# A fourth Toeplitz buffer, rotation tables from two short runs, an earlier weight split and a later spread in a two-layer decoder trunk

## The chip, the cores and the metric

The program runs on one core of a Trainium2 chip. The metric is the device time of one execution in microseconds (us). The kernel before was timed at 2249.5, 2243.65 and 2248.94 us, median 2248.94; a separate execution was profiled and took 2244.88 us. TensorE (PE) multiplies matrices, VectorE (DVE), ScalarE (ACT) and GpSimd (POOL) work elementwise, and SyncE (SP) issues most of the transfers between device memory and the on-chip buffers. Each engine, and each engine's issue queue, works in the order of its own list: what waits holds back all that stands behind it.

## The reference

Two layers, each a mixer and a dense feed-forward block (FFN) with RMS norms and residual adds. The same weights serve a prompt of 1024 positions and 8 samples of 8 positions with carried state; the kernel lays both side by side as 1088 columns. All work is float32. Layer 0 mixes with a convolution module, layer 1 with a diagonal state-space scan (SSM):

```python
def conv_module(h, buf, w_pw1, b_pw1, w_dw, b_dw, ln_g, ln_b, w_pw2):
    a = h @ w_pw1 + b_pw1
    v = a[..., :D_MODEL] * jax.nn.sigmoid(a[..., D_MODEL:])
    full = jnp.concatenate([buf.astype(v.dtype), v], axis=1)
    y = lax.conv_general_dilated(full, w_dw[:, None, :], ..., feature_group_count=D_MODEL) + b_dw
    y = jax.nn.silu(layer_norm(y, ln_g, ln_b))
    return y @ w_pw2, full[:, -(CONV_WIDTH - 1):]
...
def swiglu(h, w_gate, w_up, w_down):
    return (jax.nn.silu(h @ w_gate) * (h @ w_up)) @ w_down
...
yp = yp + dp
yp = yp + swiglu(rms_norm(yp, norm_ffn[i]), w_gate[i], w_up[i], w_down[i])
```

The scan of layer 1 needs, for each of 64 groups and 64 state rows (kept as 128 lanes), powers of a complex number of unit size: 128 cosines and 128 sines per group. The kernel tabulates them while layer 0 runs; they are called rotations.

## The kernel before, in words

*Tiles.* A tile has 128 partitions and up to 1088 columns. Most large tiles (named `big`) come from one pool of 35 slots that are handed on as they come free. Weights of the pointwise products are fetched into 3 `w` slots and split into a high and a low half (`split_weight`: ScalarE writes the high half, VectorE the low one) in 6 `wg` slots; a product is then three matmuls for each 128x128 piece, high by high, high by low and low by high.

*The convolution stage* loops over channel blocks fb = 0 to 7 of 128 channels, and `depthwise` follows two blocks behind. `pointwise(fb)` makes two products (`pv`, `pg`; 72 matmuls each) and gates one with the other into `v`. `relayout(fb)` sends `v` through device memory (`vs`, then `u`) into a layout in which the depthwise convolution is a product with Toeplitz tiles. `depthwise(fb)` runs 80 matmuls `dw` with four such tiles `tz` (640 KB each, three slots); the result goes back through device memory (`ys`) into `y`. `moments` adds up the sums over blocks that the layer norm needs (`lnsum`, `lnsq`): blocks 0 to 3 are summed by VectorE and TensorE then makes the mean (`lcps`, in the middle of the product of block 7), while blocks 4 to 7 are summed in the transposed layout (`late_moments`: `late4` to `late7`, added up in `late4_0`), so that their sums can be taken (`late`, line 1218) as soon as the last depthwise product is done.

*Beside it* runs the preparation of the SSM: `ssm_parameters`; `replicate_powers`, 32 transfers `edup` issued on ScalarE's queue; and `rotations(fb)`. For each block, 44 GpSimd instructions double a run of cosines and sines from 1 to 128 entries, and two stores (`st_tc`, `st_ts`, 512 KB each, SyncE's queue) write them out.

*The second pointwise product* takes the normalised tiles `n0` to `n7` (`h` and `l` halves). Output blocks 0 to 2 are computed together, column chunk by column chunk, while the layer norm is applied; blocks 3 to 7 follow one after another (`p`), each with its own split weight. `skip_products` (line 530) puts eight copies `xrep` on ScalarE in that place. `Mixed` gathers the sums for the FFN's RMS norm, and `spread` turns the factor per column into a tile `f0r` by a product (`f0rp`) with a diagonal `f0rdg` that GpSimd makes.

*Order.* The program is written as loops and a scheduler orders each engine's list by its own cost model; `later(n)` lowers the priority of what is written under it, and `issue_after` adds an order between two instructions.

Of the kernel before, what the change touches and what calls it, by code (L numbers as in the profile page):

```python
# [8 lines left out]
F32 = mybir.dt.float32  # L9
F32R = mybir.dt.float32r  # L10
# [4 lines left out]
P = 128  # L15
D = 1024
# [3 lines left out]
L = 8  # L20
# [42 lines left out]
def decoder_kernel(ctx: ExitStack, tc: tile.TileContext, A):  # L63
# [46 lines left out]
        SP.dma_start(w, src)  # L110
        return w, name

    def split_weight(w, name, behind=None, ordered=False):
        wh = wpool.tile([P, D], F32R, tag="wg", name=f"{name}h", bufs=6)
        high = S.activation(wh, w, AF.Copy)
        if ordered:
            tc.keep_in_program_order(high)
        wl = wpool.tile([P, D], F32R, tag="wg", name=f"{name}l", bufs=6)
        with tc.issue_after(behind.ins) if behind else nullcontext():
            V.tensor_sub(wl, w, wh.bitcast(F32))  # L120
        return wh, wl
# [412 lines left out]
    def skip_products():  # L534
# [18 lines left out]
        ssm["dg"] = cpool.tile([P, G], F32, name="dg")  # L553
        V.tensor_mul(ssm["dg"], cst[:, K_DREP : K_DREP + G], cst[:, K_GREP : K_GREP + G])

    def rotations(fb):

        gs = slice(fb * GF, (fb + 1) * GF)
        tcos, tsin, t1 = [big(f"rot{fb}_{i}") for i in range(3)]
        cv, sv, tmp = [t[:, :D].rearrange("p (g n) -> p g n", n=NCK) for t in (tcos, tsin, t1)]  # L560
        GP.tensor_copy(cv[:, :, 0], ssm["zc"][:, 0, gs])
        GP.tensor_copy(sv[:, :, 0], ssm["zs"][:, 0, gs])
        for lv in range(NLV):
            k = 1 << lv
            shp = [P, GF, k]
            ck = ssm["zc"][:, lv, gs].unsqueeze(2).to_broadcast(shp)
            sk = ssm["zs"][:, lv, gs].unsqueeze(2).to_broadcast(shp)
            c0, s0 = cv[:, :, :k], sv[:, :, :k]
            c1, s1 = cv[:, :, k : 2 * k], sv[:, :, k : 2 * k]
            ta = tmp[:, :, :k]  # L570
            GP.tensor_mul(c1, c0, ck)
            GP.tensor_mul(ta, s0, sk)
            GP.tensor_sub(c1, c1, ta)
            GP.tensor_mul(s1, s0, ck)
            GP.tensor_mul(ta, c0, sk)
            GP.tensor_add(s1, s1, ta)
        SP.dma_start(ssm["tc"][fb], tcos[:, :D])
        SP.dma_start(ssm["ts"][fb], tsin[:, :D])


# [112 lines left out]
    def ffn_up(layer, name, mixed, tp, temp, extra=None):  # L693
# [82 lines left out]
        for q in range(NPR):  # L776
# [19 lines left out]
            if q == 0:  # L796
                gate = Seven(q, "gate", c, gated, True)
                u.update({w: temp() for w in ("11", "22")})
                up = Seven(q, "up", u, product, True)
                mixed.before(1)  # L800
                mixed.before(2)
                for work, i in (
                    (gate, 1), (up, 1), (gate, 2), (gate, 6), (up, 2), (up, 6), (gate, 7),
                    (gate, 5), (up, 7), (up, 5), (gate, 4), (gate, 3), (up, 4), (up, 3),
                ):
                    mixed.before(i)
                    mm = work.product(i)
                    if (work, i) == (up, 1):
                        mixed.factors(mm)
                    if (work, i) == (up, 2):  # L810
                        mixed.spread(mm)
                    if i in (7, 5, 4, 3):
                        work.finish()
                prior = up.evac
            else:
                for kind in ("gate", "up"):
                    if kind == "up":
                        u.update({w: mixed.temp() for w in ("11", "22")})
                    work = Seven(q, kind, c if kind == "gate" else u, gated if kind == "gate" else product)
                    for i in (1, 2, 6, 7, 5, 4, 3):  # L820
                        work.product(i)
                        work.finish()
                    if extra is not None:
                        extra(2 * q + (kind == "up"), prior)
                    prior = work.evac
# [216 lines left out]
    with tc.tile_pool(name="conv", bufs=2) as cv:  # L1042
# [25 lines left out]
            return v  # L1068

        def toeplitz(fb, q):  # L1070
            t = cv.tile([P, 2 * NM, C, L], F32, tag="tz", name=f"tz{fb}_{q}", bufs=3)
            SP.dma_start(t.rearrange("p k c i -> p (k c i)"), A["toep"][fb, q])
            return t

        def relayout(fb, v):
# [10 lines left out]
            tail = cv.tile([P, L, 4], F32, tag="tail", name=f"tail{fb}")  # L1086
            V.tensor_copy(tail, vj[:, :, NCOL - 4 :])
            SP.dma_start(A["vtail"][f0], tail)
            win = cv.tile([P, NB, WIN], F32, tag="win", name=f"win{fb}")
            SP.dma_start(win, A["cache"][f0])  # L1090
            V.tensor_copy(win[:, :, HIST:].rearrange("p b j -> p j b"), vj[:, :, :NB])
            SP.dma_start(A["vwin"][f0], win)
# [169 lines left out]
        for fb in range(NFB + LAG):  # L1262
# [6 lines left out]
                replicate_powers((fb - 4) * C // 2, C // 2)  # L1269
            if fb < NFB:  # L1270
                staged.append(relayout(fb, pointwise(fb)))
            for k in {2: (0,), 3: (1, 2), 4: (3,), 5: (4, 5), 6: (6,), 7: (7,)}.get(fb, ()):
                rotations(k)
            if fb >= LAG:
                k = fb - LAG
                if k == NFB - LATE:
# [81 lines left out]
    with ExitStack() as st:  # L1358
# [4 lines left out]
        for ci in range(len(CH)):  # L1363
# [5 lines left out]
            if ci == 0:  # L1369
                for fb in range(NFB):  # L1370
                    xt.append(big(f"xr{fb}"))
                    loaded = SP.dma_start(xt[fb], A["xT"][fb * P : (fb + 1) * P])
            if ci == 2:
                skip_products()
            for fb in range(ahead):
# [4 lines left out]
            mixed.feed(fb)  # L1380
        for fb in range(ahead, NFB):
            t = xt[fb]
            w = load_weight(A["pw2"][fb], f"pw2_{fb}")
            ps = banks(f"p2_{fb}")
            for k in range(NFB):
                product(ps, w, kcols(k), yn[k], k == 0, k == NFB - 1)
# [460 lines left out]
```

## Time and profile before

| | |
|---|---|
| Timed runs | 2249.5, 2243.65, 2248.94 us |
| Median | 2248.94 us |
| Profiled execution | 2244.88 us |
| Its span | 2243.1 us |
| TensorE busy | 2135.5 us (95%) |
| VectorE busy | 1658.1 us (74%) |
| GpSimd busy | 993.5 us (44%) |
| ScalarE busy | 805.2 us (36%) |

The span runs from the first instruction's start to the last one's end. Busy times are of one profiled execution; an engine that is busy 95% of the span can only be made to end sooner where its idle time, or work of its own, goes. The convolution stage takes the span up to about 340 us, and the second pointwise product ends at about 461 us.

### The profile page before, as it was taken

What the parts mean: (1) busy time and instruction counts of PE and PEld (TensorE: products, weight loads), DVE (VectorE), ACT (ScalarE), POOL (GpSimd) and SP (SyncE); (2) the same over time, 40 slices, a digit from 0 to 9 for tenths busy, and PEclk for the clock granted to TensorE, in tenths of its full rate; (3) what the DMA queues carried; (4) which work ended last, traced back from release to release, by engine and by line L of the source; (5) the groups of instructions that cost most, each with busy time, mean ns of one, the idle gap of its engine ahead of it and who ended that gap; (6) DMA issues with size and microseconds to landing.
All of it is one profiled execution on the core that took longest, in us unless ns stands there. A gap on an engine that the chain in (4) does not pass through costs nothing.

```text
span 2243.1 us, 39882 instructions
## 1 busy us (share of the span) xinstructions
PE 2135.5 (95%) x15760; PEld 2102.7 (94%) x15760; DVE 1658.1 (74%) x2552; ACT 805.2 (36%) x1538; POOL 993.5 (44%) x953
## 2 busy tenths in 40 slices
PE   8998879889999999999998989998999999999997
PEld 7998878889999999999998889998999999999997
DVE  7975877688799999987585973339676766787586
ACT  4201125343333333333363542225333333333462
POOL 3367864455366667645131121126343343355133
PEclk9999888989999999999999999998999999999998
DMA  5479383413444455487295862211322322388542
GB/s 216 152 235 317 122 261 143 175 39 106 146 161 165 165 170 196 149 309 275 85 344 186 286 221 104 88 59 39 127 92 78 122 92 74 138 292 309 166 126 80
DMA packets 200731, 370.73 MB, mean 165 GB/s; under 512 B 16224, under 2 KB 91104, under 8 KB 200544
## 3 DMA queue, kind: packets, MB, share of 16 engines
q1 hardware_dynamic: 175328, 355.34, 45.4%
q10 hardware_dynamic: 25216, 12.85, 2.1%
q8 instruction: 123, 2.02, 0.4%
q14 instruction: 64, 0.52, 0.1%
HBM read 259.34 MB, written 108.79 MB: 164 GB/s over the span
## 4 chain that ended last, share of the span: by engine, by line
PE 69%; DVE 17%; issue 4%; DMA 4%; POOL 2%; ACT 2%; ACTq 1%; SPq 0%; DVEq 0%; POOLq 0%
PE f1d L600 10%; PE f0d L600 9%; PE gg L131 4%; PE gv L131 4%; PE p L131 4%; PE pv L131 3%; PE pg L131 2%; PE dw L1116 2%; DVE r L1529 1%; DVE b L529 1%; PE f1up4m L600 1%; PE f0up7m L600 1%; PE f1gate10m L600 1%; PE f1up9m L600 1%; PE f1gate9m L600 1%
## 5 line engine op out<-in xcount | busy, mean ns | idle before, releaser
L600 PE MATMUL f0d<-f0db,f0da 128*128 128x272 f32 x1848 | 234.4, 289 | 2.5 <-DVE f0db L593 2.3
L600 PEld LDWEIGHTS f0d<-f0db,f0da 128*128 128x128 f32 x1848 | 232.5, 188 | 3.4 <-DVE f0db L593 3.1
L600 PE MATMUL f1d<-f1db,f1da 128*128 128x272 f32 x1848 | 234.6, 289 | 0.8 <-DVE f1db L593 0.4
L600 PEld LDWEIGHTS f1d<-f1db,f1da 128*128 128x128 f32 x1848 | 232.7, 188 | 1.7 <-DVE f1db L593 1.0
L593 DVE TENSOR_TENSOR f1db<-f1b,f1db 128x544 fp32r<-128x544 f32 x77 | 74.2, 971 | 40.8 <-ACT f1db L592 40.8
L593 DVE TENSOR_TENSOR f0db<-f0b,f0db 128x544 fp32r<-128x544 f32 x77 | 69.6, 912 | 39.0 <-ACT f0db L592 38.4
L1116 PE MATMUL dw<-u,tz 128*128 128x128 f32 x640 | 81.4, 289 | 14.7 <-DMA tz<-in_toep 14.7
L1116 PEld LDWEIGHTS dw<-u,tz 128*128 128x128 f32 x640 | 79.0, 204 | 16.3 <-DMA tz<-in_toep 14.1
L592 ACT ACTIVATE f0db<-f0b 128x544 fp32r<-128x544 f32 x77 | 49.9, 654 | 97.6 <-PE f0d L600 81.7
L592 ACT ACTIVATE f1db<-f1b 128x544 fp32r<-128x544 f32 x77 | 49.9, 653 | 91.0 <-PE f1d L600 88.5
L593 DVE TENSOR_TENSOR f0da<-f0a,f0da 128x512 fp32r<-128x512 f32 x77 | 71.7, 938 | 13.4 <-ACT f0da L592 13.3
L593 DVE TENSOR_TENSOR f1da<-f1a,f1da 128x512 fp32r<-128x512 f32 x77 | 72.4, 949 | 6.8 <-ACT f1da L592 4.1
L1657 DVE SCALAR_TENSOR_TENSOR gs<-gv,cst,gs 128x408 f32<-128x408 f32 (+1 forms) x24 | 12.8, 589 | 68.4 <-PE gv L131 68.0
L235 POOL TENSOR_TENSOR f1acc<-f1acc,f1t 128x544 f32<-128x544 f32 x10 | 13.4, 1366 | 109.7 <-ACT f1t L234 109.7
L235 POOL TENSOR_TENSOR f1nacc<-f1nacc,f1nsq 128x544 f32<-128x544 f32 (+1 forms) x13 | 16.6, 1283 | 94.1 <-ACT f1nsq L234 93.9
L235 POOL TENSOR_TENSOR f0nacc<-f0nacc,f0nsq 128x544 f32<-128x544 f32 (+1 forms) x13 | 15.5, 1210 | 92.9 <-ACT f0nsq L234 92.8
L529 DVE SCALAR_TENSOR_TENSOR b<-kr,cst,b 128x448 f32<-128x448 f32 (+6 forms) x112 | 54.3, 485 | 0.6
L491 POOL TENSOR_TENSOR b<-b,b 128x512 f32<-128x512 f32 x32 | 53.8, 1699 | 1.2
L787 ACT ACTIVATE f1t<-f1t 128x544 f32<-128x544 f32 x44 | 28.8, 655 | 70.8 <-DVE f1t L786 54.6
L592 ACT ACTIVATE f0da<-f0a 128x512 fp32r<-128x512 f32 x77 | 46.9, 619 | 20.2 <-DMA f0a<-in_down 5.8
L592 ACT ACTIVATE f1da<-f1a 128x512 fp32r<-128x512 f32 x77 | 47.2, 621 | 17.3 <-POOL f1a L876 7.3
L787 ACT ACTIVATE f0t<-f0t 128x544 f32<-128x544 f32 x44 | 28.8, 656 | 66.7 <-DVE f0t L786 57.0
(3127 smaller groups left out, 6366.6 us busy)
## 6 DMA issues: line engine op xcount, KB each, us to landing
f0b<-td SPq DMA_DIRECT2D x77, 272.0 KB, 6.6
f1b<-td SPq DMA_DIRECT2D x77, 272.0 KB, 5.4
tz<-in_toep SPq DMA_DIRECT2D x32, 640.0 KB, 6.8
f0a<-in_down SPq DMA_DIRECT2D x40, 512.0 KB, 7.1
f1a<-in_down SPq DMA_DIRECT2D x40, 512.0 KB, 5.9
td<-f0t SPq DMA_DIRECT2D x22, 544.0 KB, 5.8
td<-f1t SPq DMA_DIRECT2D x22, 544.0 KB, 5.2
f0gate<-in_gate SPq DMA_DIRECT2D x22, 512.0 KB, 4.1
```

The costliest lines, as they stand in the source:

```text
L131: PE.matmul(ps[c][:, :n], a, b[:, o : o + n], start=first and i == 0, stop=last and i == 2)
L235: self.last = E.tensor_add(acc, acc, t[:, :n])
L491: GP.tensor_mul(v, v, b.unsqueeze(2).to_broadcast([P, GU, 2, PS]))
L529: V.scalar_tensor_tensor(tv[:, :, s:], kv[:, :, : L - s], col(K_MJ, s), tv[:, :, s:], op0=ALU.mult, op1=ALU.add)
L592: S.activation(out[:, :n], x, AF.Copy)
L593: EL.tensor_sub(out[:, n : 2 * n], x, out[:, :n].bitcast(F32))
L600: mm = PE.matmul(ps[s - at][:, :QT], a[:, ah * an + ac : ah * an + ac + P], b[:, bo : bo + QT], start=first and i == 0, stop=last and i == ...
L787: S.activation(c[w], c[w], AF.Silu)
L1116: ln["dw"] = PE.matmul(ps[:, g * P : (g + 1) * P], tz[:, (g % 2) * NM + m].rearrange("p c i -> p (c i)"), uv[:, h * GU + g, PADC - m : PAD ...
L1529: V.tensor_tensor_scan(rtv[:, k], ssm["m8"][:, g0 + k : g0 + k + 1].to_broadcast([P, NCK]), rotv[:, k], 0.0, op0=ALU.mult, op1=ALU.add,)
L1657: V.scalar_tensor_tensor(sg[:, o : o + n], p[:, :n], col(K_BGV, fb), sg[:, o : o + n], op0=ALU.add, op1=ALU.mult)
```

## The change

Four edits:

1. The Toeplitz tiles have four slots in place of three (`win`, a small tile of cached inputs, pays with one slot in place of two).
2. The rotations are no longer doubled out block by block on GpSimd. `rotation_bases`, run once during block 2, makes for all 64 groups a run of 16 (`cb`, `sb`) and a run of 8 with the stride of 16 (`ca`, `sa`): 46 GpSimd instructions. `rotations(fb)` then forms the 128 entries of each group as products of an entry of the one run and an entry of the other: six VectorE instructions of 128x1024 for a block, both inputs of a product read with a broadcast. It is called in blocks 3 to 7 in place of 2 to 7, under `later(100)`.
3. The weight of output block 3 of the second pointwise product is fetched and split while blocks 0 to 2 are computed; its halves lie in `big` slots (`full=True`).
4. In the FFN's first column part, the spread of the ratio is written after the sixth product of `up` in place of the second.

```diff
-    def split_weight(w, name, behind=None, ordered=False):
-        wh = wpool.tile([P, D], F32R, tag="wg", name=f"{name}h", bufs=6)
+    def split_weight(w, name, behind=None, ordered=False, full=False):
+        def half(nm):
+            return big(nm, F32R)[:, :D] if full else wpool.tile([P, D], F32R, tag="wg", name=nm, bufs=6)
+
+        wh = half(f"{name}h")
...
-        wl = wpool.tile([P, D], F32R, tag="wg", name=f"{name}l", bufs=6)
+        wl = half(f"{name}l")
...
+    NA, NI = 8, 16
+
+    def rotation_bases():
+
+        runs, cb, sb, tmp = [big(f"rb{i}") for i in range(4)]
+        ca, sa = [runs[:, i * G * NA : (i + 1) * G * NA].rearrange("p (g n) -> p g n", n=NA) for i in range(2)]
...
+        for c, s, n, lv0 in ((cb, sb, NI, 0), (ca, sa, NA, 4)):
+            lv, k = lv0, 1
+            while k < n:
...
+                GP.tensor_mul(c1, c0, ck)
+                GP.tensor_mul(ta, s0, sk)
+                GP.tensor_sub(c1, c1, ta)
+                GP.tensor_mul(s1, s0, ck)
+                GP.tensor_mul(ta, c0, sk)
+                GP.tensor_add(s1, s1, ta)
+                lv, k = lv + 1, 2 * k
+        ssm.update(ca=ca, sa=sa, cb=cb, sb=sb)
+
     def rotations(fb):
 
         gs = slice(fb * GF, (fb + 1) * GF)
+        shp = [P, GF, NA, NI]
         tcos, tsin, t1 = [big(f"rot{fb}_{i}") for i in range(3)]
-        cv, sv, tmp = [t[:, :D].rearrange("p (g n) -> p g n", n=NCK) for t in (tcos, tsin, t1)]
-        GP.tensor_copy(cv[:, :, 0], ssm["zc"][:, 0, gs])
-        GP.tensor_copy(sv[:, :, 0], ssm["zs"][:, 0, gs])
-        for lv in range(NLV):
...
-            GP.tensor_mul(c1, c0, ck)
-            GP.tensor_mul(ta, s0, sk)
-            GP.tensor_sub(c1, c1, ta)
-            GP.tensor_mul(s1, s0, ck)
-            GP.tensor_mul(ta, c0, sk)
-            GP.tensor_add(s1, s1, ta)
+        cv, sv, tmp = [t[:, :D].rearrange("p (g a b) -> p g a b", a=NA, b=NI) for t in (tcos, tsin, t1)]
+        ca, sa = [ssm[z][:, gs].unsqueeze(3).to_broadcast(shp) for z in ("ca", "sa")]
+        cb, sb = [ssm[z][:, gs].unsqueeze(2).to_broadcast(shp) for z in ("cb", "sb")]
+        V.tensor_mul(cv, ca, cb)
+        V.tensor_mul(tmp, sa, sb)
+        V.tensor_sub(cv, cv, tmp)
         SP.dma_start(ssm["tc"][fb], tcos[:, :D])
+        V.tensor_mul(sv, sa, cb)
+        V.tensor_mul(tmp, ca, sb)
+        V.tensor_add(sv, sv, tmp)
         SP.dma_start(ssm["ts"][fb], tsin[:, :D])
...
-                    if (work, i) == (up, 2):
+                    if (work, i) == (up, 6):
                         mixed.spread(mm)
...
-            t = cv.tile([P, 2 * NM, C, L], F32, tag="tz", name=f"tz{fb}_{q}", bufs=3)
+            t = cv.tile([P, 2 * NM, C, L], F32, tag="tz", name=f"tz{fb}_{q}", bufs=4)
...
-            win = cv.tile([P, NB, WIN], F32, tag="win", name=f"win{fb}")
+            win = cv.tile([P, NB, WIN], F32, tag="win", name=f"win{fb}", bufs=1)
...
-            for k in {2: (0,), 3: (1, 2), 4: (3,), 5: (4, 5), 6: (6,), 7: (7,)}.get(fb, ()):
-                rotations(k)
+            if fb == 2:
+                rotation_bases()
+            for k in {3: (0, 1), 4: (2,), 5: (3, 4), 6: (5,), 7: (6, 7)}.get(fb, ()):
+                with later(100):
+                    rotations(k)
...
+            if ci == 1:
+                next_w = split_weight(*fetch_weight(A["pw2"][ahead], f"pw2_{ahead}"), full=True)
...
-            w = load_weight(A["pw2"][fb], f"pw2_{fb}")
+            w = next_w if fb == ahead else load_weight(A["pw2"][fb], f"pw2_{fb}")
```

How the change moves instructions, at three places. The first is SyncE's queue around the depthwise product of block 2 (`tz2_0` to `tz2_3` are its Toeplitz tiles, `st_tc1` the cosine table of block 1, `win4` belongs to block 4). The kernel before:

```order
L1072 DMA tz2_2_1862<-in_toep 128x1280
L1090 DMA win5_2086<-in_cache 128x304
L1138 DMA ys1_1498<-yu1_1497 128x4x128
L1141 DMA y1_885<-ys1_1498 64x8x128 x2
L577 DMA st_tc1_686<-rot1_0_1399 128x1024
L1072 DMA tz2_3_1874<-in_toep 128x1280
L1080 DMA vs4_1757<-v4_1747 1024x1x128
```

and the changed kernel:

```order
L1095 DMA tz2_1_1733<-in_toep 128x1280
L1095 DMA tz2_2_1749<-in_toep 128x1280
L1107 DMA u3_1377<-vs3_1375 128x8x128
L1095 DMA tz2_3_1761<-in_toep 128x1280
L1161 DMA ys1_1423<-yu1_1422 128x4x128 x2
L597 DMA st_tc0_685<-rot0_0_1400 128x1024
L597 DMA st_tc1_686<-rot1_0_1411 128x1024
L1164 DMA y1_885<-ys1_1423 64x8x128 x2
L601 DMA st_ts0_693<-rot0_1_1401 128x1024
L601 DMA st_ts1_694<-rot1_1_1412 128x1024
L1113 DMA win4_1690<-in_cache 128x304
L1095 DMA tz3_0_2015<-in_toep 128x1280
```

The tile `tz2_3`, which stood behind the store of a rotation table, now stands ahead of the four stores of blocks 0 and 1, which come together there with `tz3_0` behind them.

The second place is VectorE's list after the gated product of the last block (`prod7` and `y7` are its samples, `late5` and `late4_0` the transposed sums). The kernel before:

```order
L1101 TENSOR_TENSOR prod7_0_2841<-win7_2836,cst_75 128x496
L1102 TENSOR_REDUCE y7_2840<-prod7_0_2841 128x2x8
L1101 TENSOR_TENSOR prod7_2_2844<-win7_2836,cst_75 128x496
L1102 TENSOR_REDUCE y7_2840<-prod7_2_2844 128x2x8
L1185 TENSOR_TENSOR late5_0_2938<-yu5_2907,cs_2550 128x4x128
L1101 TENSOR_TENSOR prod7_4_2847<-win7_2836,cst_75 128x496
L1192 TENSOR_TENSOR late4_0_2613<-late4_0_2613,late5_0_2938 128x544
L1102 TENSOR_REDUCE y7_2840<-prod7_4_2847 128x2x8
L1192 TENSOR_TENSOR late4_0_2613<-late4_0_2613,late5_0_2938 128x544
```

and the changed kernel (`rot6`, `rot7` are the last two blocks' rotations, `rb0` to `rb2` the short runs):

```order
L1124 TENSOR_TENSOR prod7_0_2614<-win7_2609,cst_75 128x496
L1125 TENSOR_REDUCE y7_2613<-prod7_0_2614 128x2x8
L594 TENSOR_TENSOR rot6_0_2626<-rb0_1095,rb1_1096 128x1024
L595 TENSOR_TENSOR rot6_2_2628<-rb0_1095,rb2_1097 128x1024
L598 TENSOR_TENSOR rot6_1_2627<-rb0_1095,rb1_1096 128x1024
L594 TENSOR_TENSOR rot7_0_2637<-rb0_1095,rb1_1096 128x1024
L595 TENSOR_TENSOR rot7_2_2639<-rb0_1095,rb2_1097 128x1024
L598 TENSOR_TENSOR rot7_1_2638<-rb0_1095,rb1_1096 128x1024
L1124 TENSOR_TENSOR prod7_2_2617<-win7_2609,cst_75 128x496
L1208 TENSOR_TENSOR late5_0_2684<-yu5_2653,cs_2323 128x4x128
L596 TENSOR_TENSOR rot6_0_2626<-rot6_0_2626,rot6_2_2628 128x1024
L1208 TENSOR_TENSOR late5_1_2721<-yu5_2653,cs_2323 128x4x128
```

The twelve instructions of `rot6` and `rot7` stand between the sample products and the transposed sums; the first seven of them are among these rows.

The third place is ScalarE's list around the layer norm's last column chunk and the second pointwise product (`n0h` to `n7h` are the normalised halves, `pw2_3h` the high half of the weight of block 3). The kernel before:

```order
L1343 ACTIVATE n7h_3248<-y7_2840 128x272
L234 ACTIVATE f0t1_3724<-xr1_3505 128x544
L547 ACTIVATE xrep0_3686<-skip0_3675 128x1024
L547 ACTIVATE xrep8_3689<-skip0_3675 128x1024
L547 ACTIVATE xrep16_3692<-skip0_3675 128x1024
L547 ACTIVATE xrep24_3695<-skip0_3675 128x1024
L547 ACTIVATE xrep32_3698<-skip0_3675 128x1024
L547 ACTIVATE xrep40_3701<-skip0_3675 128x1024
L547 ACTIVATE xrep48_3704<-skip0_3675 128x1024
L547 ACTIVATE xrep56_3707<-skip0_3675 128x1024
L230 ACTIVATE f0acc_3716<-xr0_3503 128x544
L115 ACTIVATE pw2_3h_3747<-pw2_3_3745 128x1024
```

and the changed kernel:

```order
L1369 ACTIVATE n0h_2980<-y0_426 128x272
L1368 ACTIVATE y3_1387<-y3_1387,cst_75 128x272
L1369 ACTIVATE n1h_2982<-y1_885 128x272
L118 ACTIVATE pw2_3h_3345<-pw2_3_3343 128x1024
L1368 ACTIVATE y4_1694<-y4_1694,cst_75 128x272
L1369 ACTIVATE n2h_2984<-y2_1082 128x272
L1368 ACTIVATE y5_1977<-y5_1977,cst_75 128x272
L1369 ACTIVATE n3h_2986<-y3_1387 128x272
L1368 ACTIVATE y6_2255<-y6_2255,cst_75 128x272
L1368 ACTIVATE y7_2613<-y7_2613,cst_75 128x272
L1369 ACTIVATE n4h_2988<-y4_1694 128x272
```

`pw2_3h` stood behind the eight `xrep` copies; it now stands among the last chunk's activations.

## Rows read from the trace of the kernel before

**Rows 1.** The page: span; busy time and share of TensorE.
```profile
span 2243.1 us, 39882 instructions
...
PE 2135.5 (95%) x15760; PEld 2102.7 (94%) x15760; DVE 1658.1 (74%) x2552; ACT 805.2 (36%) x1538; POOL 993.5 (44%) x953
```
**Rows 2.** TensorE's waits, 100 to 600 us: who, for what: total us, times, longest.
```profile
PE dw L1116 <- DMA tz<-in_toep: 14.7, 7, 5.3
PE lcps L161 <- DVE lnsum L1234: 9.7, 1, 9.7
PE p L131 <- ACT pw_3h L115: 5.8, 1, 5.8
PE ln L1201 <- DVE lnsum L1170: 4.4, 1, 4.4
PE f0rp L200 <- POOL f0rdg L187: 3.9, 1, 3.9
```
**Rows 3.** TensorE's timeline: start us, us, instruction, count, [idle before <- releaser].
```profile
180.13 4.63 PE L1116 MATMUL dw<-u,tz 128*128 128x128 f32 x20 [5.28 <-DMA tz<-in_toep]
189.54 0.66 PE L131 MATMUL pg<-c0h,pg5h 128*128 128x408 f32 x3
...
215.33 2.50 PE L1116 MATMUL dw<-u,tz 128*128 128x128 f32 x20 [1.56 <-DMA tz<-in_toep]
...
246.12 3.76 PE L161 MATMUL lcps<-ones,lnsum 128*68 128x1 f32 x32 [9.67 <-DVE lnsum L1234]
...
288.00 0.66 PE L131 MATMUL pg<-c7h,pg7l 128*128 128x408 f32 x3
...
484.97 1.17 PE L600 MATMUL f0up0m<-f0b,f0up0a 128*128 128x272 f32 x8
```
**Rows 4.** SyncE's queue, 165 to 175 us, columns as in rows 3.
```profile
171.57 0.34 SPq L1072 DMA_DIRECT2D tz<-in_toep  x1
```
**Rows 5.** ScalarE's timeline, around 184 and around 398 us.
```profile
183.84 1.06 ACT L115 ACTIVATE pg5h<-pg 128x1024 fp32r<-128x1024 f32 x1 [5.74 <-DMA edup<-epowT]
...
397.77 1.04 ACT L115 ACTIVATE pw_3h<-pw 128x1024 fp32r<-128x1024 f32 x1
```
**Rows 6.** DMA queue of SyncE, 166 to 184 us: packets, MB, share of 16 engines.
```profile
q1 hardware_dynamic: 618, 1.35, 23.9%
```
**Rows 7.** VectorE's timeline, columns as in rows 3.
```profile
190.76 1.23 DVE L120 TENSOR_TENSOR pg6l<-pg,pg6h 128x1024 fp32r<-128x1024 f32 x1
...
225.52 19.20 DVE L120 TENSOR_TENSOR pg7l<-pg,pg7h 128x1024 fp32r<-128x1024 f32 x1
...
315.98 4.05 DVE L1192 TENSOR_TENSOR late<-late,late 128x544 f32<-128x544 f32 x2
...
340.65 1.40 DVE L1192 TENSOR_TENSOR late<-late,late 128x544 f32<-128x544 f32 x2
...
384.67 1.22 DVE L540 TENSOR_TENSOR skip<-skip,sk 128x1024 f32<-128x1024 f32 x1
```
**Rows 8.** GpSimd's timeline: first and last of 22 such rows, 225 to 244 us.
```profile
225.67 0.61 POOL L571 TENSOR_TENSOR rot<-rot,zc 128x256 f32<-128x256 f32 x1
...
242.38 1.26 POOL L576 TENSOR_TENSOR rot<-rot,rot 128x512 f32<-128x512 f32 x1
```
**Rows 9.** The chain that ended last, in order of time: start us, us, what.
```profile
81.73 12.00 PE pg L131 x72
...
249.88 14.14 PE pv L131 x72
...
341.62 2.29 PE late L1218 x32
...
398.87 62.47 PE p L131 x358
```
**Rows 10.** Windows: us, busy of PE, PEld, DVE, ACT, POOL, PE clock, DMA share, GB/s.
```profile
120.00:289.00 169.00, 152.49 (x1004) 150.72 (x1003) 117.51 (x139) 25.50 (x35) 133.41 (x267) 0.94 0.73 227
289.00:342.00 53.00, 40.15 (x314) 37.87 (x314) 36.31 (x51) 14.80 (x41) 29.73 (x51) 0.84 0.78 249
```

More of the change, by code (lines that the diff above doesn't have):

```diff
@@ L554, in skip_products @@
         V.tensor_mul(ssm["dg"], cst[:, K_DREP : K_DREP + G], cst[:, K_GREP : K_GREP + G])
+    NA, NI = 8, 16
+    def rotation_bases():
+        runs, cb, sb, tmp = [big(f"rb{i}") for i in range(4)]
+        ca, sa = [runs[:, i * G * NA : (i + 1) * G * NA].rearrange("p (g n) -> p g n", n=NA) for i in range(2)]
+        cb, sb = [t[:, : G * NI].rearrange("p (g n) -> p g n", n=NI) for t in (cb, sb)]
+        GP.memset(ca[:, :, 0], 1.0)
+        GP.memset(sa[:, :, 0], 0.0)
+        GP.tensor_copy(cb[:, :, 0], ssm["zc"][:, 0])
+        GP.tensor_copy(sb[:, :, 0], ssm["zs"][:, 0])
+        for c, s, n, lv0 in ((cb, sb, NI, 0), (ca, sa, NA, 4)):
+            lv, k = lv0, 1
+            while k < n:
+                shp = [P, G, k]
+                ck, sk = [ssm[z][:, lv].unsqueeze(2).to_broadcast(shp) for z in ("zc", "zs")]
+                ta = tmp[:, : G * k].rearrange("p (g n) -> p g n", n=k)
+                c0, s0, c1, s1 = c[:, :, :k], s[:, :, :k], c[:, :, k : 2 * k], s[:, :, k : 2 * k]
+                GP.tensor_mul(c1, c0, ck)
[6 more added lines that the diff above has]
+        ssm.update(ca=ca, sa=sa, cb=cb, sb=sb)
@@ L556, in rotations @@
     def rotations(fb):
         gs = slice(fb * GF, (fb + 1) * GF)
+        shp = [P, GF, NA, NI]
         tcos, tsin, t1 = [big(f"rot{fb}_{i}") for i in range(3)]
-        cv, sv, tmp = [t[:, :D].rearrange("p (g n) -> p g n", n=NCK) for t in (tcos, tsin, t1)]
-        GP.tensor_copy(cv[:, :, 0], ssm["zc"][:, 0, gs])
-        GP.tensor_copy(sv[:, :, 0], ssm["zs"][:, 0, gs])
-        for lv in range(NLV):
[L564 to L570, printed above, removed]
-            GP.tensor_mul(c1, c0, ck)
-            GP.tensor_mul(ta, s0, sk)
-            GP.tensor_sub(c1, c1, ta)
-            GP.tensor_mul(s1, s0, ck)
-            GP.tensor_mul(ta, c0, sk)
-            GP.tensor_add(s1, s1, ta)
+        cv, sv, tmp = [t[:, :D].rearrange("p (g a b) -> p g a b", a=NA, b=NI) for t in (tcos, tsin, t1)]
```

## The prediction

> **What bounds the kernel now.** I read the page first: TensorE is busy for 2135.5 of 2243.1 us [rows 1], so the end moves only by what TensorE waits for, or by what the clock loses after a wait. The list of TensorE's waits between 100 and 600 us comes next, since the edits lie there. Five entries make up most of it [rows 2]: Toeplitz tiles (14.7 us in seven waits), the sum `lnsum` before the layer norm's mean (9.7), the weight half `pw_3h` (5.8), the same sum before the layer norm's end (4.4) and the diagonal `f0rdg` (3.9), together 38.5 us. Each of the four edits touches at least one. TensorE's timeline then gives their places, and what follows each: after the 5.28 us wait at 180.13, 20 `dw` matmuls take 4.63 us, where the same 20 take 2.50 at 215.33 [rows 3]. The slow start costs 2.1 us on top. Last I read the chain of waits, for the stages as they run on the path: a product of 72 matmuls takes 12.00 us undisturbed, 14.14 around the `lnsum` wait, and blocks 3 to 7 of the second product take 62.47 [rows 9].
>
> I call T the end of the product `pg7`, 288.7 us by its last matmuls [rows 3]. Up to T TensorE sets the pace; from T to the `late` matmuls, whose row ends at 343.9 [rows 9], it is busy only 40.15 of 53 us at a granted clock of 0.84, against 0.94 before [rows 10], and what it waits for there is a list of VectorE work and transfers. So the two stretches are summed apart.
>
> **The change part by part.**
>
> *Block 5's start.* The tile `tz2_3` is issued at 171.57 [rows 4], behind the store of `rot1` in SyncE's order (first place of the change), and TensorE starts on it at 180.13. In the new order it stands ahead of the stores and has a slot of its own, so the 5.28 and the 2.1 us go: TensorE would be ready for `pg5` at 189.5 - 7.4 = 182.1. But `pg5` needs `pg5h`, which ScalarE starts at 183.84, having waited 5.74 us for the `edup` transfers that its own queue issues ahead of it [rows 5]; in the new order it stands behind all 32 of them as before. Those share the 16 engines with SyncE's queue, and that queue gets three more table stores (0.52 MB each) and one more `tz` (0.66 MB) in this stretch. SyncE's queue moved 1.35 MB in 23.9% of 18 us [rows 6], 3.2 us for a MB with all engines; 2.2 MB more is 7 us. I take 6.8: `pg5h` ends at 191.7 and `pg5` starts 2.3 us later than before, and the 9 us wait leaves a slow start of its own, 2.3 us by the 2.1 above. That is +4.6. The other end is that the stores find room and nothing of the gain is lost: -7.4. I take +4.6, because the engines' queue in that stretch is the one row that shows them shared.
>
> *Other Toeplitz waits before T.* The one at 215.33, 1.56 us [rows 3], goes with the fourth slot: -1.6. The remaining five of the seven lie behind T and are part of the tail. The single `win` slot makes the next block's `win` load wait for this block's sample products; it is 128x304 and is needed only after the next gate, about 24 us later (two products), so I put it at nothing. If that cover is gone it delays samples alone, which have slack until the tail.
>
> *The sum `lnsum`.* The low half `pg7l` takes 19.20 us on VectorE, its sister `pg6l` 1.23 [rows 7]. Over just that stretch GpSimd runs 22 rotation instructions in a row, ending with one of 1.26 us at 242.38 [rows 8]; VectorE gets on when they end. `lnsum` stands behind `pg7l`, and TensorE waits 9.67 us for it [rows 3]. With the doubling gone from GpSimd, the low half should take 1.2 us. The wait goes (-9.67), and the product around it returns from 14.14 to 12.00 (-2.1). A new wait can appear: `y3`, the last term of the sum, now passes SyncE behind stores of rotations 3 and 4 and its tile `yu3` follows a rotation's slot. I give it 1 us, between 0 and 5. Together -10.8.
>
> The Trainium skill, page "SBUF — State Buffer", section "Who interferes with whom", says that VectorE with two inputs and GpSimd share one pair of ports under an exclusive lock, which is held for one instruction and fully blocks the other engine. By that rule alone `pg7l` would be held up by one GpSimd instruction, 1.26 us at the longest here [rows 8], and the 18 us must have another cause, which the change need not remove; the row shows VectorE shut out for the whole run of them, so that the lock was granted to GpSimd again and again, and removal of the run removes the 18 us. I follow the row; the rule's outcome is the third rival.
>
> *What the rotations cost on VectorE.* 48 instructions of 128x1024. None with two broadcast inputs of this size is in the trace; the nearest, with one broadcast input, takes 1.22 us at 384.67 [rows 7]: 58.6 us in all. From below it can hardly be under 1.2 (the same number of elements), from above I allow 1.5 (72 us). 36 of them, 44 us, come before T. There VectorE is busy 117.5 of 169 us [rows 10], and that contains 18 us of `pg7l`'s lost time; about 100 + 44 = 144 of 160 fit, under low priority. Nothing on the path, if the order is kept, and +44 if none of it were covered. The bases, 46 GpSimd instructions, run once when no other GpSimd work is due; nothing.
>
> *The tail from T.* Before: T + 55.2 (343.9 - 288.7). VectorE has 36.31 us of work there [rows 10], part of it stretched by GpSimd's 29.73: a pair of `late` additions takes 4.05 us at 315.98 and 1.40 at 340.65 [rows 7]. At unstretched durations the 51 instructions come to about 29 us (an estimate, shape by shape from such rows). The twelve rotation instructions that now stand in this list (second place of the change) add 12 x 1.22 = 14.6. 29 + 14.6 + 2.3 for the `late` matmuls [rows 9] + 1 to 2 for hand-overs is T + 47: -8. If the stretching stayed, 36.3 + 14.6 + 3 = 54, -1; if the transfers let the rotations slide beside other work, -11. I take -8, since the stretch belongs to GpSimd's rotations. The waits for `lnsum` (4.4) and for `tz` in this stretch are inside the -8, not beside it.
>
> *The weight of block 3.* `pw_3h` runs at 397.77 [rows 5], behind the eight `xrep` copies, and TensorE waits 5.8 us [rows 2]. Moved among the last chunk's activations (third place of the change), it is done long before. The wait goes, and the five blocks return from 62.47 [rows 9] to 5 x 12.00, another -2.5: together -8.3. The two more instructions in the layer norm's lists (about 1.0 us on ScalarE, 1.2 on VectorE) may push the last chunk by as much; and the `xrep` copies may now delay `pw_4h`, which has 12 us of cover. Bounds -8.3 to -5.
>
> *The spread of the ratio.* It moves by six matmuls of 1.17/8 = 0.15 us [rows 3]: of the 3.9 us wait, 0.7 to 0.9 go; -0.7. Bounds -3.9 to 0.
>
> **Sum.** +4.6 - 1.6 - 10.8 - 8 - 8.3 - 0.7 = -24.8 us against the profiled execution's 2244.88 (span 2243.1 and 1.8 around it): 2220.1. That execution is 4.1 under the median of the runs shown, which scatter from 2243.65 to 2249.5, so I add half of it: 2222.
>
> **The rivals.**
>
> *First, the stores find room* (chance 0.22). `edup` ends no later than before, and block 5 gains up to 7.4 in place of losing 4.6: 12 us better, 2210. For it: the last `edup` copies are few and the extra stores could run behind them. Against it: they are issued from two queues to the same engines.
>
> *Second, VectorE becomes late itself* (0.17). 144 of 160 us leave little room, and low priority is decided by a cost model ahead of time, not while the kernel runs. If `lnsum` comes 5 us late (and the clock costs 2.3 again, in place of the 1 us above: +6.3) and the tail keeps 2 of its 8 us (+6), the sum is -12.5: 2234, up to 2243. For it: the rows of VectorE in the tail; against it: GpSimd no longer stretches them.
>
> *Third, the stretch on VectorE is not GpSimd's doing* (0.05). Then neither `pg7l` nor the tail gains, -10.8 and -8 go, and -6 is left: 2241.
>
> *Fourth, slower* (0.08). The rotation products stand ahead of low weight halves and sums in VectorE's order and fall on the path before T. Of the 44 us there, 31 would have to be uncovered to bring the sum to the +6.7 above the median that counts as slower (24.8 + 6.7 = 31.5); all 44 give 2266. For it: VectorE runs in order, and a product waiting for its slot holds what is behind it. Against it: TensorE's list of waits names no low half before T [rows 2], and the products need just short runs that have long been ready.
>
> **How the numbers follow.** My forecast has 0.48, with its own range of 2213 to 2231; the four rivals 0.22, 0.17, 0.05 and 0.08. Adding the bounds of the parts gives 2206 at the low end (-7.4 - 1.6 - 11.8 - 11 - 8.3 - 0.7 = -40.8) and about 2241 at the high one, which takes in the first and third rival and most of the second. 0.3%, 6.7 us, is about what a measurement of this kernel can tell from no change. Faster than 2242.2 are the forecast, the first, most of the second and half of the third: 0.82; within it 0.10; slower 0.08.
>
> **What would show it.** In the changed kernel's profile: `pg7l` at about 1.2 us and the `lcps` wait under 2; no wait for `tz` in blocks 2, 3 and 5, but a wait of about 9 us for `pg5h` on ScalarE before `pg5`; rotation instructions of 1.2 us on VectorE; the `late` matmuls ending 47 us after `pg7`; no wait for `pw_3h`, and 60 us for the five blocks; a wait for `f0rdg` of about 3. I am wrong if TensorE waits for low weight halves in blocks 3 to 7, if `pg5` starts without a wait, or if the tail keeps its 55 us.

## The result and the profile after

The changed kernel was timed at 2230.4 us (median of six, 2222.31 to 2239.01) against 2247.7 us for the kernel before in the same session: a ratio of 0.9919, 95% interval 0.9892 to 0.9947. The forecast of the time was 2222, so the gain of the medians is 17.3 us where about 27 were expected. The profiled execution has a span of 2228.0 us, 15.1 less than before; the forecast summed to 24.8 less.

The page of the changed kernel, first and second entry, as in [rows 1]:

```profile
span 2228.0 us, 39622 instructions
...
PE 2129.6 (96%) x15760; PEld 2098.3 (94%) x15760; DVE 1668.5 (75%) x2600; ACT 805.8 (36%) x1538; POOL 846.6 (38%) x647
```

TensorE's waits between 100 and 600 us, columns as in [rows 2]:

```profile
PE pg L134 <- ACT pg5h L118: 11.8, 1, 11.8
PE dw L1139 <- DMA tz<-in_toep: 10.6, 5, 3.6
PE f0gate0m L623 <- DVE f0b L616: 5.0, 2, 4.5
PE lnr L1344 <- issue: 3.3, 1, 3.3
...
PE lcps L164 <- DVE lnsum L1257: 1.0, 1, 1.0
```

Of the five entries of [rows 2], both for `lnsum`, the one for `pw_3h` and the one for `f0rdg` are gone or small. Tiles still cost 10.6 us, all of it behind `pg7`, and the waits for `pg5h` and for the low half `f0b` are new. TensorE's timeline shows where each stands:

```profile
191.72 1.28 PE L134 MATMUL pg<-c0h,pg5h 128*128 128x408 f32 x3 [11.75 <-ACT pg5h L118]
...
241.18 2.17 PE L164 MATMUL lcps<-ones,lnsum 128*68 128x1 f32 x32 [0.99 <-DVE lnsum L1257]
...
279.23 0.66 PE L134 MATMUL pg<-c7h,pg7l 128*128 128x408 f32 x3
...
317.84 4.13 PE L1139 MATMUL dw<-u,tz 128*128 128x128 f32 x20 [3.63 <-DMA tz<-in_toep]
324.04 2.92 PE L1224 MATMUL ln<-ones,lnsum 128*68 128x1 f32 x32
326.83 3.77 PE L1224 MATMUL ln<-ones,lnsq 128*68 128x1 f32 x32
331.50 3.73 PE L1241 MATMUL late<-cst,late 128*68 128x8 f32 x32
...
444.14 2.42 PE L623 MATMUL f0gate0m<-f0b,f0gate0a 128*128 128x272 f32 x18
...
474.81 1.73 PE L623 MATMUL f0gate0m<-f0b,f0gate0a 128*128 128x272 f32 x6 [4.46 <-DVE f0b L616]
476.33 2.92 PE L203 MATMUL f0rp<-f0rdg,ones 68*128 68x408 f32 x4
```

Set against the same places of before, stage by stage (us of each profiled execution; the differences add to the 15.1):

| stage, to | before | after | difference | forecast |
|---|---|---|---|---|
| T, end of `pg7` | 288.7 | 279.9 | -8.8 | -7.8 |
| end of `late` | 55.2 later | 55.3 later | +0.1 | -8 |
| end of the second product | 117.6 later | 108.9 later | -8.7 | -8.3 |
| start of `f0gate1m` | 58.6 later | 59.8 later | +1.2 | -0.7 |
| end of the span | 1723.0 later | 1724.1 later | +1.1 | 0 |

T and the second product stand within about 1 us of the forecast. The tail, the stretch from T to the end of the `late` matmuls, gave nothing where 8 us were expected; that is the question for the experiments. VectorE's timeline, `pg7l` first and then the tail:

```profile
230.28 1.22 DVE L123 TENSOR_TENSOR pg7l<-pg,pg7h 128x1024 fp32r<-128x1024 f32 x1
...
292.29 1.22 DVE L594 TENSOR_TENSOR rot<-rb,rb 128x1024 f32<-128x1024 f32 x1
...
323.04 0.22 DVE L1193 TENSOR_TENSOR lnsum<-lnsum,y 128x64 f32<-128x64 f32 x1
323.38 0.23 DVE L1193 TENSOR_TENSOR lnsq<-lnsq,lsq 128x64 f32<-128x64 f32 x1
323.52 1.45 DVE L1215 TENSOR_TENSOR late<-late,late 128x544 f32<-128x544 f32 x2
```

VectorE's list ends at 324.97, T + 45.1, near the 29 + 14.6 = 43.6 of the forecast, but VectorE is busy for only 38.7 us of that and waits for the rest. The samples' last additions to `lnsum` and `lnsq` now come at 323.04 and 323.38, behind the rotations, and the 64 `ln` matmuls that read them (324.04 to 330.60) can only start about then. So 6.6 us of TensorE work stand behind VectorE's list, with TensorE's clock granted at 0.57 of full speed, and the `late` matmuls behind them take 3.73 us at 0.50. In the kernel before, the `ln` matmuls ran between the depthwise products, and the `late` ones took 2.45 us at 0.83:

```profile
314.35 3.79 PE L1201 MATMUL ln<-ones,lnsum 128*68 128x1 f32 x32 [4.37 <-DVE lnsum L1170]
...
326.21 0.60 PE L1201 MATMUL ln<-ones,lnsq 128*68 128x1 f32 x8
...
341.45 2.45 PE L1218 MATMUL late<-cst,late 128*68 128x8 f32 x32
```

VectorE's list did not set the end of the tail there. Of the 55.2 us it was idle for 17.9, and its last `late` terms waited for ScalarE and TensorE:

```profile
327.58 0.69 DVE L1185 TENSOR_TENSOR late<-yu,cs 128x512 f32<-128x512 f32 x1 [5.62 <-ACT yu L1134]
...
339.42 1.13 DVE L1181 SCALAR_TENSOR_TENSOR late<-dw,cst,cs 128x128 f32<-128x128 f32 x4 [4.63 <-PE dw L1116]
```

### The profile page after: what moved, and what is told of

Same layout as the page of the kernel before. It is cut to its first block, busy times and chain, and to the rows that moved or that the text cites. A ratio compares the mean times of both kernels' runs of the same rounds, so it can differ in the third digit from the quotient of the medians.

```text
span 2228.0 us, 39622 instructions
## 1 busy us (share of the span) xinstructions
PE 2129.6 (96%) x15760; PEld 2098.3 (94%) x15760; DVE 1668.5 (75%) x2600; ACT 805.8 (36%) x1538; POOL 846.6 (38%) x647
## 4 chain that ended last, share of the span: by engine, by line
PE 68%; DVE 18%; DMA 6%; issue 4%; ACTq 1%; ACT 1%; POOL 1%; SPq 1%; DVEq 0%; POOLq 0%
PE f1d L623 10%; PE f0d L623 9%; PE p L134 4%; PE gg L134 4%; PE gv L134 4%; PE pv L134 2%; PE pg L134 1%; ACTq L462 1%; DVE r L1557 1%; DVE b L532 1%; PE f0gate3m L623 1%; PE f1gate2m L623 1%; PE f1gate10m L623 1%; PE f1up9m L623 1%; PE f1gate9m L623 1%
## 5 line engine op out<-in xcount | busy, mean ns | idle before, releaser
L1139 PE MATMUL dw<-u,tz 128*128 128x128 f32 x640 | 77.0, 283 | 10.7 <-DMA tz<-in_toep 10.6
L810 ACT ACTIVATE f1t<-f1t 128x544 f32<-128x544 f32 x44 | 28.8, 656 | 71.3 <-DVE f1t L809 55.3
L494 POOL TENSOR_TENSOR b<-b,b 128x512 f32<-128x512 f32 x32 | 53.8, 1700 | 1.2
L615 ACT ACTIVATE f1da<-f1a 128x512 fp32r<-128x512 f32 x77 | 47.2, 621 | 17.3 <-POOL f1a L899 7.3
L810 ACT ACTIVATE f0t<-f0t 128x544 f32<-128x544 f32 x44 | 28.8, 655 | 65.8 <-DVE f0t L809 55.2
```

The source lines that it names most:

```text
L494: GP.tensor_mul(v, v, b.unsqueeze(2).to_broadcast([P, GU, 2, PS]))
L615: S.activation(out[:, :n], x, AF.Copy)
L810: S.activation(c[w], c[w], AF.Silu)
L1139: ln["dw"] = PE.matmul(ps[:, g * P : (g + 1) * P], tz[:, (g % 2) * NM + m].rearrange("p c i -> p (c i)"), uv[:, h * GU + g, PADC - m : PAD ...
```

## The experiments

Each kernel below was timed beside the kernel before, and the ratio to it, with its 95% interval, is what compares two sessions; the changed kernel's is 0.9919 (0.9892 to 0.9947). Differences in us are differences of the medians. One trace was taken of each kernel. From the start of `f0gate1m` to the end of the span the traces of the kernels here differ by up to 6 us (1722.8 in `both_moves`, 1728.8 in `u_rot`), though no edit is made there, so the stages before it say more of an edit than the total does.

**Parts undone.** Each kernel takes one edit out of the changed kernel.

`u_rot`: the function `rotations` (not printed here) and its calls are those of before.

```diff
...
-            if fb == 2:
-                rotation_bases()
-            for k in {3: (0, 1), 4: (2,), 5: (3, 4), 6: (5,), 7: (6, 7)}.get(fb, ()):
-                with later(100):
-                    rotations(k)
+            for k in {2: (0,), 3: (1, 2), 4: (3,), 5: (4, 5), 6: (6,), 7: (7,)}.get(fb, ()):
+                rotations(k)
```

> The changed kernel with the rotations doubled out block by block on GpSimd again, the other three edits kept. Theory (GpSimd's runs shut VectorE out): low weight halves of about 19 us are back beside them, the wait for the sum in the product of block 7 grows from 1.0 to 8 to 10 us, and the time rises by 9 to 13 us over the changed kernel. Rival (the fourth Toeplitz slot and the new order of transfers removed that wait): it stays under 3 us, and the time moves by less than 3.

2234.81 us, ratio 0.9945 (0.9925 to 0.9965), 4.4 us over the changed kernel, with intervals that overlap; the forecast rise of 9 to 13 was missed, though the wait came back larger than expected. Its TensorE timeline:

```profile
245.32 3.76 PE L164 MATMUL lcps<-ones,lnsum 128*68 128x1 f32 x32 [15.98 <-DVE lnsum L1264]
...
287.88 0.66 PE L134 MATMUL pg<-c7h,pg7l 128*128 128x408 f32 x3
...
332.38 2.84 PE L1248 MATMUL late<-cst,late 128*68 128x8 f32 x32
```

and on VectorE the sum itself is now what is stretched:

```profile
218.40 1.23 DVE L123 TENSOR_TENSOR pg7l<-pg,pg7h 128x1024 fp32r<-128x1024 f32 x1
...
228.62 16.55 DVE L1264 SCALAR_TENSOR_TENSOR lnsum<-y,cst,lnsum 128x1088 f32<-128x1088 f32 x1 [9.00 <-DMA y<-ys]
```

Another instruction is caught than in the kernel before, where it was `pg7l`; beside shorter rotation instructions `pg7l` now takes 1.23 us. T comes 8.65 us later than in the changed kernel, but the tail is 46.7 us (335.2 - 288.5) in place of 55.3, and both reach the second product at the same time (`lnr` at 338.49 in each). In these traces the rotations on VectorE save 8.65 us before T and give 8.6 back behind it, so by itself this edit gains nothing up to there. The rest of the difference arises later, with more waits for `f0t` on ScalarE in the FFN, and was not followed up.

The tail of `u_rot` says more. GpSimd's rotations are back in it (30.02 us of 289 to 342, against the 29.73 of [rows 10]), and yet it is 8.5 us shorter than before. TensorE's waits for tiles are 3.2 us there, in one wait, against 7.9 in the five of before:

```profile
PE dw L1146 <- DMA tz<-in_toep: 3.2, 1, 3.2
```

So the other edits shorten the tail with GpSimd's stretch in place. The fourth slot is the likely one; no run here takes it alone.

`u_tz`: three Toeplitz slots and two `win` slots.

```diff
-            t = cv.tile([P, 2 * NM, C, L], F32, tag="tz", name=f"tz{fb}_{q}", bufs=4)
+            t = cv.tile([P, 2 * NM, C, L], F32, tag="tz", name=f"tz{fb}_{q}", bufs=3)
...
-            win = cv.tile([P, NB, WIN], F32, tag="win", name=f"win{fb}", bufs=1)
+            win = cv.tile([P, NB, WIN], F32, tag="win", name=f"win{fb}")
```

> The changed kernel with three Toeplitz slots and two small input tiles again. Theory (the gain at block 5 is swallowed, since the second product there starts only when its weight half comes out behind the replicating transfers, at 191.7 us): the start of that product stays within 2 us of 191.7, and the time rises by 0 to 4 us. Rival (the fourth slot pays by itself): the waits for Toeplitz tiles before the last block come back in full, 5.3 + 2.1 + 1.6 us, and the time rises by 7 to 10.

2231.28 us (0.9929, 0.9908 to 0.9949), 0.9 more. In its timeline the tiles cost 16.5 us of waits in place of 10.6, yet:

```profile
194.90 0.80 PE L134 MATMUL pg<-c0h,pg5h 128*128 128x408 f32 x3 [4.24 <-ACT pg5h L118]
```

The product starts 3.2 us later than with four slots (a little over the 2 us expected), and T is 0.4 us later. What the tile costs is taken off the wait for `pg5h`: beside the other edits the fourth slot is worth nothing that can be measured.

`u_split`: the weight of block 3 in its old place.

```diff
-            if ci == 1:
-                next_w = split_weight(*fetch_weight(A["pw2"][ahead], f"pw2_{ahead}"), full=True)
...
-            w = next_w if fb == ahead else load_weight(A["pw2"][fb], f"pw2_{fb}")
+            w = load_weight(A["pw2"][fb], f"pw2_{fb}")
```

> The changed kernel with the weight of output block 3 fetched and split in its old place. Theory: TensorE waits about 6 us for the high half behind the eight copies and starts slowly, so that the five blocks take 68 to 69 us and the time rises by 8 to 9. Rival (ScalarE comes to the copies earlier now, or the early split takes something from the layer norm that is given back here): it rises by less than 5.

2238.96 us (0.9961, 0.9947 to 0.9976), 8.6 more, as expected, and the intervals just touch. In its trace, of the quickest of its eight executions, the second product takes 8.0 us longer, while the tail ends 3.4 earlier than in the changed kernel, which was not followed up. The wait of [rows 2] is back to the tenth:

```profile
PE p L134 <- ACT pw_3h L118: 5.8, 1, 5.8
```

`u_spread`: `(up, 2)` in place of `(up, 6)`.

> The changed kernel with the spread of the ratio after the second product of up again. Theory (the later place costs, since six matmuls now stand ahead of the spread that need a low half which VectorE has not made): the wait of 4.5 us moves back to the spread itself, at 3.9 us, and the gate product of the next column part starts 0.5 to 2 us earlier; the time falls by 0 to 2. Rival (the later place pays as forecast): the time rises by 0.5 to 2.

2231.23 us (0.993, 0.9906 to 0.9955): no difference that can be told. In the trace the wait moves as the theory has it:

```profile
474.16 3.09 PE L203 MATMUL f0rp<-f0rdg,ones 68*128 68x408 f32 x4 [3.68 <-POOL f0rdg L190]
```

and `f0gate1m` starts 0.9 us earlier after the second product's end. The six gate matmuls that now stand ahead of `f0rp` need a low half `f0b`, which VectorE makes while GpSimd builds `f0rdg`; they wait longer than the spread did. The times of the runs cannot tell a difference of this size.

**The tail: matmuls or transfers.** `samples_first` puts the samples of block 7 ahead of the last two blocks' rotations:

```diff
+                if fb == NFB - 1:
+                    for r in (6, 7):
+                        with later(100), tc.issue_after(ln["sampled"].ins):
+                            rotations(r)
```

> The changed kernel with the sample products of block 7 and their sums put ahead of the twelve rotation instructions of blocks 6 and 7 on VectorE, so that the 64 matmuls for the norm's sums of blocks 0 to 3 can run between the depthwise products; the instructions are the same in number. Theory (the tail lost its gain because those 64 matmuls stand behind the last depthwise product, 6.6 us, and start slowly): the tail from the last gated product to the last late matmul falls from 55.3 to 47 to 50 us, and the time by 5 to 8. Rival (transfers set the tail): it stays within 2 us.

2222.22 us (0.9897, 0.9865 to 0.9929), 8.2 under the changed kernel by the medians, about 5 by the ratios, whose intervals overlap. The trace is clearer. TensorE's timeline:

```profile
275.98 0.66 PE L134 MATMUL pg<-c7h,pg7l 128*128 128x408 f32 x3
...
294.50 3.79 PE L1224 MATMUL ln<-ones,lnsum 128*68 128x1 f32 x32 [8.93 <-DVE lnsum L1193]
298.15 1.27 PE L1224 MATMUL ln<-ones,lnsq 128*68 128x1 f32 x10
...
314.25 1.46 PE L1224 MATMUL ln<-ones,lnsq 128*68 128x1 f32 x22
...
323.33 2.11 PE L1241 MATMUL late<-cst,late 128*68 128x8 f32 x32
```

The same 64 matmuls run between the depthwise products, the `late` ones take 2.11 us at a granted clock of 1.00 and end at 325.4, and the tail is 48.8 us, as the theory had it. T itself comes 3.3 us earlier, which the theory does not explain. The order shows in the other traces too: `both_moves` and `both_on_sp` below, with the samples first, have tails of 50.0 and 50.3 us, while `u_tz`, `u_split`, `u_spread`, `no_stores` and `edup_later`, which keep the changed kernel's order, have 53.8 to 57.6 us (behind the long stall of `combined` and `edup_pool` it is 50.6 against 53.0).

`no_stores` leaves out the four table stores of blocks 6 and 7 (`if fb < 6:` ahead of the stores), so that layer 1 reads the table of block 5 for them.

> The changed kernel without the four table stores of blocks 6 and 7 (2 MB; layer 1 then reads the table of block 5 in their place); all engine work is the same. Rival theory (the stores crowd the Toeplitz tiles in the tail): the waits for tiles there fall from 10.6 us to under 5 and the tail from 55.3 to under 50, the time by over 5. Theory of the 64 matmuls: the list on VectorE and the matmuls behind it still set the end, the tail loses 0 to 3 us.

2228.33 us (0.9922, 0.9899 to 0.9945): no difference that can be told. The waits for tiles fall from 10.6 to 7.9 us, and the tail does not shrink:

```profile
278.97 0.66 PE L134 MATMUL pg<-c7h,pg7l 128*128 128x408 f32 x3
...
324.93 3.79 PE L1229 MATMUL ln<-ones,lnsum 128*68 128x1 f32 x32 [1.93 <-DVE lnsum L1198]
328.57 3.77 PE L1229 MATMUL ln<-ones,lnsq 128*68 128x1 f32 x32
332.20 3.77 PE L1246 MATMUL late<-cst,late 128*68 128x8 f32 x32
```

It ends at 336.0, 56.3 us after T. With 2 MB less to move, what TensorE no longer waits for tiles it waits for `lnsum`. The table stores as the tail's bound are ruled out; the loads of the tiles remain in it. That the order of VectorE's list costs the tail about 6 us is shown by `samples_first`.

**The wait for `pg5h`.** Four kernels take the 32 `edup` transfers off the place ahead of it. `edup_pool` changes only the queue:

```diff
-                S.dma_start(
+                GP.dma_start(
                     ed[r, c].rearrange("j g h -> g j h"),
```

> The changed kernel with the 32 replicating transfers issued on GpSimd's queue in place of ScalarE's; TensorE's order is the same. Theory (the 11.8 us wait before the second product of block 5 is ScalarE's queue, in which the weight half stands behind those transfers): the half is made by 180, the wait goes or is under 3 us, and the time falls by 8 to 13. Rival (the transfers load the 16 engines whatever the queue, and the weight itself or the tiles come late then): the wait moves to a tile or a weight and the time falls by less than 4.

2290.2 us (1.0196, 1.0169 to 1.0223): much slower. The wait for `pg5h` is gone (`pg5` starts at 181.89 without one), so ScalarE's queue was its cause; but:

```profile
292.74 1.34 PE L134 MATMUL pv<-c0h,pv7h 128*128 128x408 f32 x3 [65.76 <-DVE v L1085]
```

and on VectorE:

```profile
201.76 1.22 DVE L598 TENSOR_TENSOR rot<-rb,rb 128x1024 f32<-128x1024 f32 x1
279.34 1.22 DVE L594 TENSOR_TENSOR rot<-rb,rb 128x1024 f32<-128x1024 f32 x1 [76.36 <-DMA edup<-epowT]
```

GpSimd issues one transfer in 3.3 us or more, the last at 276.22. VectorE's next rotation waits for these transfers, which read `epowT`: by the code its tile (`rot4`) takes over that slot of `big`. What is behind it in VectorE's list waits too, the evacuation of the products among it. Neither theory had this.

`combined` is that kernel with the samples first and the old spread.

> The changed kernel with the samples first, the replicating transfers on GpSimd's queue, and the spread after the second product of up. If the three waits are independent, as the theory has it, the falls add up: 14 to 22 us under the changed kernel, 2208 to 2217. If the transfers are the common limit, under 8 us.

2284.95 us (1.0166, 1.0133 to 1.02): the same stall (65.6 us), so the run says nothing on whether the gains add up.

`edup_later` keeps them on ScalarE's queue, eight at a time in the second product:

```diff
+            if fb > ahead:
+                with tc.issue_after(highs["at"].ins):
+                    replicate_powers((fb - ahead - 1) * 4, 4)
```

> The changed kernel with the 32 replicating transfers still on ScalarE's queue, but eight at a time behind the weight halves of output blocks 4 to 7 of the second pointwise product, so outside the convolution stage; their source tile keeps its slot for 250 us longer. Theory (the 11.8 us wait before the second product of block 5 is ScalarE's queue behind these transfers): the wait goes or stays under 2 us, T comes 10 to 13 us earlier, and the time falls by 6 to 13, what is lost being the halves 5 to 7 and the copies behind eight transfers each (8 to 11 us, under the 12 us of a block). Rival (the convolution stage is bound by its transfers or by VectorE with the rotations, and the wait only moves): T comes less than 5 us earlier.

2234.54 us (0.9915, 0.9895 to 0.9934): the ratio of the changed kernel. T comes early by more than expected, at 263.8, 16.1 us before that of the changed kernel:

```profile
180.04 0.66 PE L136 MATMUL pg<-c0h,pg5h 128*128 128x408 f32 x3
...
263.11 0.67 PE L136 MATMUL pg<-c7h,pg7l 128*128 128x408 f32 x3
```

and by the end of the second product nearly all of it is lost. The weight halves, copies and activations on ScalarE now stand behind the transfers there, and TensorE waits for additions into the residual:

```profile
PE p L136 <- DVE xr L1419: 10.9, 2, 9.0
```

`both_moves` adds the samples first to that kernel.

> The changed kernel with the sample products first and the replicating transfers in the second pointwise product. If the two waits are independent: 8 us from the samples, measured, and 6 to 13 from the transfers, so 2208 to 2217. If an earlier T only makes the tail longer, since its transfers and VectorE's list are then the limit: 2217 to 2223.

2228.04 us (0.9885, 0.9861 to 0.9909), about 7.6 us under the changed kernel by the ratios, where 8 from the samples and 6 to 13 from the transfers were to add up. 12.0 us of that wait stand in the second product.

`both_on_sp` issues them on SyncE's queue instead, behind the residual's loads:

```diff
-                S.dma_start(
+                SP.dma_start(
...
+            with tc.issue_after(loaded.ins):
+                c0 = (fb - ahead) * C // (NFB - ahead)
+                replicate_powers(c0, (fb - ahead + 1) * C // (NFB - ahead) - c0)
```

> As the kernel with both moves, but with the 32 replicating transfers issued on SyncE's queue behind the loads of the residual, so that ScalarE has none of them in the second pointwise product. Theory (the gain of 16 us by T was lost again to weight halves and additions behind ScalarE's queue, 9 to 12 us of waits for additions into the residual): those waits go or stay under 3 us, and the ratio to the kernel before falls from 0.9885 to 0.980 to 0.985. Rival (the transfers take that time from the stage in whatever queue they stand): the ratio stays above 0.987.

2210.16 us (0.9836, 0.9818 to 0.9855), clearly faster than the kernel before and the changed one, and no wait for `pg5h`, tiles or additions is left among the long ones:

```profile
PE ln L1224 <- DVE lnsum L1193: 10.0, 1, 10.0
PE f0gate0m L623 <- DVE f0b L616: 4.8, 2, 4.3
PE lnr L1346 <- issue: 2.2, 1, 2.2
```

The transfers are not only in another queue: they also start about 40 us earlier, at 322.3 in place of 363.7 in `both_moves`. How much of the 11 us between the two ratios (0.9836 against 0.9885) comes from the queue and how much from the earlier place is not separated.

The Trainium skill, page "DMA: Bandwidth & Descriptors", section "Issuing engines are not separate DMA queues", says that all transfers end on the same 16 engines and that another issuing engine saves only issue time, usually small. No run here isolates the first half. The second leaves out what counts here, where the engine also computes: in the changed kernel ScalarE's queue takes 39.53 us to issue 25 of these transfers, and its activations stand behind them.

```profile
141.10 39.53 ACTq L462 DMA_DIRECT2D edup<-epowT  x25
```

## Why the prediction was right, and where it was not

The time, 2230.4 us, lies inside the stated range, at the upper edge of the forecast's own 2213 to 2231. One of the six terms is wrong by 8 us: the tail. The prediction had named it as a sign of being wrong that the tail keeps its 55 us, and it kept 55.3.

*Block 5's start* (+2.3 forecast, before a slow start): right. `pg5` began at 191.72 against 191.8, behind `pg5h`, whose row shows the transfers ahead of it:

```profile
186.87 3.70 ACTq L462 DMA_DIRECT2D edup<-epowT  x2
190.61 1.06 ACT L118 ACTIVATE pg5h<-pg 128x1024 fp32r<-128x1024 f32 x1 [3.17 <-issue]
```

The first rival (no loss there) fell with it. That the extra stores are what made it late was not isolated; with rotations on GpSimd (`u_rot`) `pg5` started at 182.57, which fits.

*The sum `lnsum`* (-10.8): right. `pg7l` took 1.22 us, the wait 0.99. The third rival, that the stretch on VectorE is not GpSimd's doing, fell too: `u_rot` brings a stretch of 16.55 us back.

*The rotations on VectorE*: right, 1.22 us each (292.29 above), covered before T.

*The tail* (-8): wrong, in two steps. The first is what sets it. The prediction took VectorE's list, stretched by GpSimd, as what made the tail 55.2 us; but VectorE was idle for 17.9 us of it, and `u_rot` has a tail of 46.7 us with GpSimd as busy as before. That the list then ended within 1.5 us of the sum (45.1 against 43.6) is luck, since it is 38.7 us of work and 6.4 of waiting. The second is the end of the sum, "2.3 for the `late` matmuls": it left out that the 64 `ln` matmuls wait for the same list once the samples stand behind the rotations. They cost 6.6 us and a slower `late`, and `samples_first` gives 6.5 of the tail back. This is the tail half of the second rival; its other half, an `lnsum` that comes 5 us late, did not happen (0.99 us).

*The weight of block 3* (-8.3): right, -8.7 in the trace, and 8.6 by the medians when it is undone.

*The spread* (-0.7): a small miss. The stage took 1.2 us more; the wait was not shortened by six matmuls but moved to their low half.

The sum was forecast at -24.8; with the tail at +0.1 and the FFN's start at +1.2 it would have been -14.8, and the trace shows -15.1. That it comes so near is in part luck, since T came 1.0 us better and the rest of the span 1.1 us worse.

## What to carry to other kernels

A list that ends in time is not enough: ask for each addition moved in it which matmuls wait for that one, and whether they still have other work to hide behind. Before a list is taken as what bounds a stretch, look at its engine's idle time there. Transfers issued on an engine that also computes hold that engine's work; put a burst of them on a queue with nothing behind it that is wanted soon. An earlier T and a shorter tail both reached the end of the program only when the transfers also left ScalarE's queue and started earlier (`both_on_sp`).

## What the runs showed of the hardware

VectorE was shut out for a whole run of GpSimd instructions again, 16.55 us in `u_rot`, not for one. Not every VectorE instruction beside such a run is caught: `pg7l` took 1.23 us in that trace. Plain transfers of 256 KB from GpSimd's queue took 3.3 us each from issue to issue in the later, steady part of `edup_pool`, with GpSimd shown idle for 2.6 of them:

```profile
272.93 0.69 POOL L462 DMA_DIRECT2D edup<-epowT  x1 [2.59 <-issue]
276.22 0.69 POOL L462 DMA_DIRECT2D edup<-epowT  x1 [2.60 <-issue]
```

ScalarE's queue issued one in 1.2 to 1.9 us in the changed kernel (25 in 39.53 us, 5 in 6.05, 2 in 3.70).
